# Differential attention: preparation of a half head in another order, weight loads over two tiles, a smaller descriptor scratch

## The chip, the cores and the metric

The kernel is one program on one core of a Trainium2 chip. The metric is the device time in microseconds of one execution. A kernel is executed several times; the time that counts is the median, and one further execution is recorded by the hardware profiler.

The engines are named as in the profile: PE is TensorE (matrix products, and transposes, which are products with an identity), DVE is VectorE, ACT is ScalarE, POOL is GpSimd, SP is SyncE, whose queue issues the transfers. PSUM is the memory that TensorE writes; it has eight banks, SBUF is the large on-chip memory.

## What is computed

One decoder layer on x of 1024 positions by 1024 channels, in float32. Three branches start from the same normalised h: an mLSTM, a differential attention and a cross-attention into 256 memory tokens. Each is projected to 1024 channels, multiplied by a sigmoid gate that is itself a projection of h, and summed; then an output projection and an MLP with squared ReLU. The change touches the differential attention and the gates:

```python
q = rms_norm(q, q_g); k = rms_norm(k, k_g)             # 8 heads, 2 components of 64 each
s = einsum('bhcqd,bhckd->bhcqk', q, k) * d ** -0.5     # causal
p = softmax(s)
a = p[:, :, 0] - lam * p[:, :, 1]                      # difference of the two components
o = einsum('bhqk,bhkv->bhqv', a, v)                    # v: 128 wide
o = rms_norm(o, subln_g) * (1 - lam_init)
g_m, g_d, g_c = split(sigmoid(h @ w_gate + b_gate), 3)
```

## The kernel before

Every float32 product is made of three products of a cheaper kind: both operands are split into a high part (a cast on ScalarE) and a low part (a subtraction on VectorE, L112), and high x high, high x low, low x high are added in one PSUM bank (`mm3`). Transposes go through PSUM in the same way, and their results are split as they are read out.

The program runs in stages: cross-attention, mLSTM, three passes of gates alone, the differential attention (`branch_d`, some 570 to 1190 us), the rest of the gates, and then output projection and MLP. TensorE's order in `branch_d` is written out by hand: all its instructions are kept in program order (`pin`), and the order on the other engines follows from the scheduler's priorities. The work is woven by a generator. `d_gemm` yields after each **step**, which is one of the eight 128-row slices k of a projection tile: three matmuls of 128x384. A tile is 128 positions of a head's q, k and v; four tiles are a half head (512 positions), and 16 half heads are 64 tiles. The loop of `branch_d` runs over 64 **attention steps** s, one block of 128 queries each. Each s makes two groups of scores (`sc`, one per component), the combination, the transposes of the block before (`tp`), and the product with the values (`po`) of the block before that. Between these pieces `fill(n)` puts n steps of projection, eight per s. When the projections are exhausted, `fill` takes gate steps instead.

After four tiles of a half head, `prep` returns five pieces with due times, in steps of the next half head. Each turn piece is four transposes (`pr` in the profile) into the *other* of the two banks `mm`, the one that the next tile will accumulate in; a cast on ScalarE and a subtraction on VectorE empty it (q: L866/L867, k: L880/L881). The piece `s_` (L874) scales the keys by their reciprocal norms on VectorE; it needs GpSimd's power of `drr` (L127, L128), which takes the sums of squares of the whole half head (L935). The line that gives the due times:

```python
return [(4, lambda: q_(0)), (12, lambda: q_(1)), (14, s_), (20, lambda: k_(0)), (28, lambda: k_(1))]
```

Each four s end with a normalisation (`norm`) in three parts: sums of squares and GpSimd's power of `dso`; the scaling on VectorE (L1054); four transposes and the result's store.

Weights of the next head are loaded and split during the last two tiles of its predecessor (`wload`, `wsplit`). Gate weights come through `gate_load` (L438 and L111/L112); the pools `wpg` (9 weight tiles) and `rpg` (2 raw tiles) serve both.

## Time and profile before

| quantity | value |
|---|---|
| median of three runs | 2282.28 us (2277.75, 2282.28, 2282.55) |
| profiled execution | 2277.11 us, span 2275.3 us |
| mean granted TensorE clock | 0.991 |
| busy: TensorE / VectorE / ScalarE / GpSimd | 2196.4 / 1395.3 / 1009.0 / 529.2 us |
| DMA queues with the kernel's data | q1 and q10, both hardware_dynamic: 233.36 and 12.58 MB |

The span is the time from the first to the last instruction. TensorE is busy in 97% of it, so its idle time, and the places where its clock is below 1, are what to look for. In a row of the timeline the bracket at the end is the idle time of that engine just before the row, and the instruction on whose end it waited. A busy time says nothing of the clock; the windows give that as a share of full speed (2.4 GHz; 0.5 is 1.2 GHz).

### The profile page before, as it was taken

The numbers are of one execution on the slowest core, as the hardware profiler recorded it, in microseconds if no ns is written. First come the engines' busy times: TensorE is split into PE (matmuls) and PEld (weight loads), VectorE is DVE, ScalarE is ACT, GpSimd is POOL, SyncE is SP. The second block draws the span as 40 slices with busy tenths as digits, with TensorE's granted clock in tenths as the row PEclk, the third lists the DMA queues.
The fourth block names the chain that finished last, engine by engine and source line by source line (L and its number), as shares of the span: only waits on it lengthen the run. The fifth ranks groups of instructions, "written<-read, shape, count | busy, mean of one in ns | idle before, by whom it ended". The sixth has DMA issues, their size and how long they took to land.

```text
span 2275.3 us, 30567 instructions
## 1 busy us (share of the span) xinstructions
PE 2196.4 (97%) x11222; PEld 1881.3 (83%) x11222; DVE 1395.3 (61%) x2627; ACT 1009.0 (44%) x1994; POOL 529.2 (23%) x696
## 2 busy tenths in 40 slices
PE   7999999999999999999899999999999999899999
PEld 5788789888899899999787888888787888688887
DVE  6636457552147877777662124353588877867789
ACT  6533445543246666666553202223345444543332
POOL 2100000000011101111000001111466766455553
PEclk9999999999999999999999999999999999999999
DMA  6022212201221100111125235434625444764444
GB/s 243 24 80 98 86 46 81 82 29 56 98 65 33 38 26 23 32 38 33 33 91 196 88 102 176 135 115 155 206 88 199 162 153 153 268 205 148 152 153 166
DMA packets 113781, 247.90 MB, mean 109 GB/s; under 512 B 11065, under 2 KB 19550, under 8 KB 111582
## 3 DMA queue, kind: packets, MB, share of 16 engines
q1 hardware_dynamic: 111326, 233.36, 30.6%
q10 hardware_dynamic: 2304, 12.58, 1.3%
q8 instruction: 88, 1.44, 0.3%
q14 instruction: 63, 0.52, 0.1%
HBM read 178.76 MB, written 67.14 MB: 108 GB/s over the span
## 4 chain that ended last, share of the span: by engine, by line
PE 73%; DVE 11%; DMA 7%; ACT 4%; issue 2%; POOL 2%; SPq 0%; DVEq 0%; ACTq 0%; POOLq 0%
PE mm L91 43%; PE p L91 21%; PE sc L91 5%; PE po L91 2%; PE tp L94 2%; ACT dpe L987 1%; DVE sc L979 1%; DVE w L112 1%; DMA raw<-in_wd 1%; DVE dpe L1000 1%; DVE daT L112 1%; DMA raw<-in_wgate 1%; DVE acc L67 1%; PE pr L94 1%; DVE dq L867 1%
## 5 line engine op out<-in xcount | busy, mean ns | idle before, releaser
L91 PE MATMUL mm<-w,hT 128*128 128x384 f32 (+3 forms) x2496 | 473.8, 331 | 13.3 <-DVE dq L867 8.7
L91 PE MATMUL mm<-hT,w 128*128 128x512 f32 x1920 | 470.4, 399 | 8.2 <-ACT w L111 6.1
L91 PEld LDWEIGHTS mm<-hT,w 128*128 128x128 f32 x1920 | 359.5, 191 | 85.1 <-ACT w L111 7.2
L91 PEld LDWEIGHTS mm<-w,hT 128*128 128x128 f32 x2496 | 387.5, 189 | 32.7 <-DVE dq L867 13.4
L91 PE MATMUL p<-xd,wo 128*128 128x512 f32 x1344 | 309.4, 392 | 5.8 <-DVE c L67 2.8
L91 PE MATMUL p<-xo,wo 128*128 128x512 f32 x1344 | 308.3, 390 | 6.0 <-DVE st L1397 1.8
L91 PEld LDWEIGHTS p<-xd,wo 128*128 128x128 f32 x1344 | 253.3, 189 | 61.8 <-DVE c L67 3.7
L91 PEld LDWEIGHTS p<-xo,wo 128*128 128x128 f32 x1344 | 251.1, 188 | 61.8 <-DVE u L67 3.7
L112 DVE TENSOR_TENSOR w<-raw,w 128x256 fp32r<-128x256 f32 (+3 forms) x304 | 172.8, 589 | 163.9 <-ACT w L111 162.7
L91 PE MATMUL mm<-kt,w 128*128 128x512 f32 x1152 | 261.3, 389 | 0.0
L91 PEld LDWEIGHTS mm<-kt,w 128*128 128x128 f32 x1152 | 216.3, 188 | 44.8
L111 ACT CAST w<-raw 128x256 fp32r<-128x256 f32 (+3 forms) x304 | 154.1, 532 | 198.4 <-PE mm L91 130.9
L104 ACT CAST wo<-wraw 128x896 fp32r<-128x896 f32 x122 | 115.0, 945 | 213.3 <-PE p L91 117.2
L67 DVE TENSOR_TENSOR wo<-wraw,wo 128x896 fp32r<-128x896 f32 x122 | 143.4, 1193 | 54.5 <-ACT wo L104 54.5
L1124 POOL TENSOR_TENSOR wraw<-wraw 128x128 f32<-128x128 f32 x128 | 92.9, 726 | 244.8 <-DMA wraw<-in_wup 86.2
L987 ACT ACTIVATE dpe<-sc,dst,drr 128x256 f32<-128x256 f32 (+7 forms) x128 | 106.7, 834 | 93.9 <-DVE dst L983 91.9
L979 DVE CUSTOM_DVE_ANT_0 sc<-sc,tmask 128x256 f32<-128x256 f32 (+7 forms) x128 | 96.9, 757 | 16.5 <-PE sc L91 16.5
L127 POOL TENSOR_SCALAR drr<-drr 128x16 f32<-128x16 f32 x16 | 3.6, 226 | 397.4 <-DVE drr L935 397.4
L1126 POOL TENSOR_TENSOR wraw<-wraw 128x128 f32<-128x128 f32 x128 | 92.2, 720 | 0.0
L1127 POOL TENSOR_TENSOR wraw<-wraw 128x128 f32<-128x128 f32 x128 | 87.2, 682 | 10.0
L127 POOL TENSOR_SCALAR hss<-hss 128x4 f32<-128x4 f32 x8 | 3.3, 409 | 356.8 <-ACT mscr L747 236.9
L91 PEld LDWEIGHTS po<-dv,daT 128*128 128x128 f32 x576 | 75.6, 193 | 11.7 <-DVE daT L112 10.2
(281 smaller groups left out, 3079.8 us busy)
## 6 DMA issues: line engine op xcount, KB each, us to landing
wraw<-in_wup SPq DMA_DIRECT2D x64, 256.0 KB, 2.9
r_d<-xts SPq DMA_DIRECT2D x16, 1024.0 KB, 4.1
wraw<-in_wdown SPq DMA_DIRECT2D x64, 256.0 KB, 3.1
xd<-r_d SPq DMA_DIRECT2D x19, 768.0 KB, 7.0
xd<-r_d SPq DMA_DIRECT2D x14, 1024.0 KB, 6.4
raw<-in_wgate SPq DMA_DIRECT2D x48, 256.0 KB, 2.8
gates<-gt SPq DMA_DIRECT2D x48, 256.0 KB, 2.0
raw<-in_wd SPq DMA_DIRECT2D x32, 384.0 KB, 3.1
```

The costliest lines, as they stand in the source:

```text
L67: return self.tc.keep_in_program_order(f(*a, **k))
L91: self.pin(self.nc.tensor.matmul(out, l, r, start=start, stop=stop))
L94: self.pin(self.nc.tensor.transpose(out, x, self.ident))
L104: self.A.copy(hi, src)
L111: nc.scalar.copy(hi, src)
L112: nc.vector.tensor_sub(lo, src, f32(hi))
L867: V.scalar_tensor_tensor(out=qT[lo, c], in0=pt[lo], scalar=self.gd[lo], in1=f32(qT[lo, c]), op0=ALU.mult, op1=ALU.subtract)
L979: V.tensor_tensor_reduce(out=sc[:, 0:n], in0=sc[:, 0:n], in1=self.tmask[:, D - n : D], scale=1.0, scalar=-3.0e38, op0=ALU.add, op1=ALU.max ...
L987: nc.scalar.activation(pe[c][:, 0:n], sc[:, 0:n], AF.Exp, bias=t8[:, 2 + c : 3 + c], scale=rr[:, i, c : c + 1], accum_out=t8[:, 4 + c : 5 ...
L1124: G.tensor_add(r[:, 4], r[:, 0], r[:, 3])
L1126: G.tensor_sub(r[:, 6], r[:, 1], r[:, 0])
L1127: G.tensor_sub(r[:, 7], r[:, 2], r[:, 5])
```

## The change

1. `gate_load` is called at every odd step of the third and fourth quarter of a pass instead of at every step of the fourth (L462).
2. `prep` has another order and other due times: first query turn at 4, scaling at 5, first key turn at 11, second query turn at 19, second key turn at 27. Tiles are handed to the attention with the first key turn. The attention starts after 60 steps instead of 64, half an attention step earlier against the tiles, and its loop runs one s longer.
3. A head's weights: three loads at the second tile's first step and a fourth after the second split; splits at the odd steps of the last two tiles. The last half head calls `gate_load` there instead.
4. At the end of the projections the remaining pieces are popped between 32 gate steps, by their due times; before, one after the other with nothing between.
5. `norm` parts 1 and 2 come one s later.
6. `wpg` has 13 buffers, `rpg` 3; the program is built with a descriptor scratch of 1024 bytes.

```diff
--- before.py
+++ after.py
@@ -459,7 +459,7 @@
                     ps = self.mm_tile()
                     for k in range(NK):
                         self.mm3(ps, (w[k][0][:, c], w[k][1][:, c]), (self.hT[:, k, 0, s], self.hT[:, k, 1, s]), k == 0, k == NK - 1)
-                        if q == 3 and r < run - 1:
+                        if q >= 2 and k % 2 and r < run - 1:
                             self.gate_load()
                         self.gdone = (g * 4 + q) * NK + k + 1
                         if k < NK - 1:
@@ -879,10 +879,10 @@
                     self.transpose(pt[:, i * P : (i + 1) * P], raws[i][:, 2 + c].rearrange("p a d -> p (a d)"))
                 nc.scalar.copy(kd[:, c], pt)
                 V.tensor_sub(kl[:, c], pt, f32(kd[:, c]))
-                if c == 1:
+                if c == 0:
                     kv.append((qT, kd, kl, vh, rr))
 
-            return [(4, lambda: q_(0)), (12, lambda: q_(1)), (14, s_), (20, lambda: k_(0)), (28, lambda: k_(1))]
+            return [(4, lambda: q_(0)), (5, s_), (11, lambda: k_(0)), (19, lambda: q_(1)), (27, lambda: k_(1))]
 
         raw = {}
 
@@ -893,19 +893,23 @@
             raw[hd, k + 1] = r[:, 384:768]
 
         def wsplit(hd, k, w):
-            if k % 2 == 0 and k < 6:
-                wload(hd, k + 2)
             t = self.wp.tile([P, 2, 384], F32R, tag="w", name=self.name("w"))
             self.split(t[:, 0], t[:, 1], raw.pop((hd, k)))
             w[k] = (t[:, 0], t[:, 1])
-
+            if k == 1:
+                wload(hd, 6)
+
+        nw = {}
         for j in range(16):
             hd, hf = divmod(j, 2)
             if j == 0:
-                w = {}
                 wload(0, 0)
+                wload(0, 2)
+                wload(0, 4)
                 for k in range(NK):
-                    wsplit(0, k, w)
+                    wsplit(0, k, nw)
+            if hf == 0:
+                w, nw = nw, {}
             rr = pool.tile([P, 4, 4], F32, tag="drr", name=self.name("drr"))
             vh, raws = [], []
             for i in range(4):
@@ -915,10 +919,14 @@
                     s = slice(t * P, (t + 1) * P)
                     self.mm3(ps, (self.hT[:, k, 0, s], self.hT[:, k, 1, s]), w[k], k == 0, k == NK - 1)
                     if hf and hd < 7:
-                        if i == 2 and k == 0:
+                        if i == 1 and k == 0:
                             wload(hd + 1, 0)
-                        if i == 3:
-                            wsplit(hd + 1, k, w)
+                            wload(hd + 1, 2)
+                            wload(hd + 1, 4)
+                        if i >= 2 and k % 2 == 1:
+                            wsplit(hd + 1, i % 2 * 4 + k // 2, nw)
+                    elif hf and i >= 2 and k % 2 == 1:
+                        self.gate_load()
                     while late and late[0][0] <= i * NK + k:
                         late.pop(0)[1]()
                     if k < NK - 1:
@@ -939,9 +947,11 @@
             self.rsqrt_mean(rl, rl, 64, 16)
             late = prep(raws, rr, vh)
             assert j < 4 or done[0] >= (j // 2 - 1) * 8
-        while late:
+        for n in range(NK * 4):
+            next(self.gates)
+            while late and late[0][0] <= n:
+                late.pop(0)[1]()
             yield True
-            late.pop(0)[1]()
 
     def branch_d(self, pool):
         nc = self.nc
@@ -1060,8 +1070,8 @@
                 nc.scalar.activation(y, pt, AF.Copy, scale=self.gsub)
                 self.store_y(1, hh // 2, hh % 2, y)
 
-        fill(64)
-        for s in range(NS + 3):
+        fill(60)
+        for s in range(NS + 4):
             hh, i = divmod(s - 2, 4)
             if s < NS:
                 scores(s, 0)
@@ -1072,12 +1082,12 @@
                     norm(hh, 0)
             if s < NS:
                 fill(2)
-            if s >= 6 and i == 1:
+            if s >= 6 and i == 2:
                 norm(hh - 1, 2)
             if s < NS:
                 scores(s, 1)
                 fill(1)
-            if s >= 6 and i == 0:
+            if s >= 6 and i == 1:
                 norm(hh - 1, 1)
             if 1 <= s < NS + 1:
                 turn(s - 1, 0)
@@ -1650,7 +1660,7 @@
                             return p.tile(shape, dt, tag=tag, name=name)
                     self.gpool, self.gwp, self.grp = T3(), self.wp, self.rp
                     self.branch_m(T3(), gm, 1)
-                with tc.tile_pool(name="wpg", bufs=9) as self.wp, tc.tile_pool(name="rpg", bufs=2) as self.rp:
+                with tc.tile_pool(name="wpg", bufs=13) as self.wp, tc.tile_pool(name="rpg", bufs=3) as self.rp:
                     self.gwp, self.grp = self.wp, self.rp
                     with tc.tile_pool(name="pg", bufs=2) as self.gpool:
                         for _ in range(3 * 32):
@@ -1730,7 +1740,7 @@
     from concourse.bass_utils import run_bass_kernel_spmd
 
     w = pack({k: np.asarray(v) for k, v in inputs.items()})
-    nc = bacc.Bacc("TRN2", target_bir_lowering=False, num_devices=1)
+    nc = bacc.Bacc("TRN2", target_bir_lowering=False, num_devices=1, dynamic_dma_scratch_size=1024)
     arrays, args = {}, {}
     for k, v in w.items():
         v = np.ascontiguousarray(v)
```

In the order of the built program: TensorE in one tile of the last but one head. `mm` is a projection step (x3: three matmuls), `pr` the turns of query or key, `tp` the turns of probabilities, `sc` scores, `po` the value product. Before, from the last of four turns on:

```order
L94 MATMUL pr_11040<-ident,draw_10815 128x128
L94 MATMUL tp_11048<-ident,dpe_10900 128x128 x2
L91 MATMUL mm_11012<-w_10781,hT 128x384 x3
L91 MATMUL mm_11012<-w_10794,hT 128x384 x3
L91 MATMUL sc_11066<-dk_10424,dq_10423 128x512
L91 MATMUL sc_11066<-dkl_10425,dq_10423 128x512
L91 MATMUL mm_11012<-w_10812,hT 128x384 x3
L91 MATMUL mm_11083<-w_10701,hT 128x384 x3
L91 MATMUL mm_11083<-w_10707,hT 128x384 x3
L91 MATMUL po_11090<-dv_10172,daT_11051 128x256
```

After, from the last of four turns on to the next tile:

```order
L94 MATMUL pr_11055<-ident,draw_10824 128x128
L91 MATMUL mm_11024<-w_10751,hT 128x384 x3
L91 MATMUL mm_11024<-w_10779,hT 128x384 x3
L91 MATMUL po_11068<-dv_10201,daT_11031 128x256
L91 MATMUL po_11068<-dv_10201,daT_11031 128x128
L91 MATMUL po_11068<-dv_10270,daT_11031 128x256
L91 MATMUL po_11068<-dv_10270,daT_11031 128x128
L91 MATMUL mm_11024<-w_10795,hT 128x384 x3
L91 MATMUL mm_11024<-w_10821,hT 128x384 x3
L91 MATMUL sc_11089<-dk_10441,dq_10440 128x512
L91 MATMUL sc_11089<-dkl_10442,dq_10440 128x512
L91 MATMUL mm_11095<-w_10645,hT 128x384 x3
```

The turn is followed by four steps, two matmul pairs of po and the scores before the next tile (another mm number) begins; before, it was three steps, the scores and tp. The transposes of the probabilities now stand behind a tile's first step.

TensorE at the end of the projections. `mm<-hT,w` with 128x512 is a step of a gate. Before:

```order
L91 MATMUL sc_11575<-dk_11168,dq_11167 128x128
L91 MATMUL sc_11575<-dkl_11169,dq_11167 128x128
L94 MATMUL pr_11581<-ident,draw_11242 128x128
L94 MATMUL pr_11581<-ident,draw_11338 128x128
L94 MATMUL pr_11581<-ident,draw_11429 128x128
L94 MATMUL pr_11581<-ident,draw_11527 128x128
L94 MATMUL tp_11588<-ident,dpe_11415 128x128 x4
L94 MATMUL pr_11596<-ident,draw_11242 128x128
L94 MATMUL pr_11596<-ident,draw_11338 128x128
L94 MATMUL pr_11596<-ident,draw_11429 128x128
L94 MATMUL pr_11596<-ident,draw_11527 128x128
L91 MATMUL mm_11635<-hT,w_11605 128x512 x3
```

After:

```order
L91 MATMUL mm_11595<-hT,w_11432 128x512 x3
L91 MATMUL sc_11627<-dk_11185,dq_11184 128x256
L91 MATMUL sc_11627<-dkl_11186,dq_11184 128x256
L91 MATMUL mm_11595<-hT,w_11456 128x512 x3
L91 MATMUL mm_11595<-hT,w_11493 128x512 x3
L94 MATMUL pr_11639<-ident,draw_11263 128x128
L94 MATMUL pr_11639<-ident,draw_11352 128x128
L94 MATMUL pr_11639<-ident,draw_11459 128x128
L94 MATMUL pr_11639<-ident,draw_11568 128x128
L91 MATMUL mm_11595<-hT,w_11521 128x512 x3
```

Before, the last groups of turns had only scores and one tp between them, and the gates began behind them; now the gates have begun, and the next group of turns stands behind their fifth step.

VectorE in the fourth tile of the second half of a head, where the next heads' weights are split (`w`). `daT` are the transposed probabilities, `dpe` of L1000 (now L1010) the combination of a block. Before:

```order
L112 TENSOR_TENSOR daT_10031<-tp_10026,daT_10031 128x512
L112 TENSOR_TENSOR w_10037<-raw_9984,w_10037 128x384
L112 TENSOR_TENSOR daT_10044<-tp_10040,daT_10044 128x384
L112 TENSOR_TENSOR w_10050<-raw_10014,w_10050 128x384
L1000 SCALAR_TENSOR_TENSOR dpe_9929<-dpe_9930,dst_9931,dpe_9929 128x1024
L983 SCALAR_TENSOR_TENSOR dst_10058<-dst_10058,drr_9340 128x1
L112 TENSOR_TENSOR w_10068<-raw_10014,w_10068 128x384
```

After:

```order
L112 TENSOR_TENSOR daT_10001<-tp_9996,daT_10001 128x512
L993 SCALAR_TENSOR_TENSOR dst_9918<-dst_9918,drr_8955 128x1
L112 TENSOR_TENSOR daT_10014<-tp_10010,daT_10014 128x384
L989 ISA sc_10026,dst_10025<-sc_10026,tmask 128x128
L989 ISA dst_10025 128x1
L112 TENSOR_TENSOR w_10035<-raw_9799,w_10035 128x384
L993 SCALAR_TENSOR_TENSOR dst_10025<-dst_10025,drr_9363 128x1
L112 TENSOR_TENSOR w_10051<-raw_9933,w_10051 128x384
L1006 RECIPROCAL dst_9918<-dst_9918 128x2
L112 TENSOR_TENSOR w_10077<-raw_9933,w_10077 128x384
L1007 SCALAR_TENSOR_TENSOR dst_9918<-dst_9918,dv 128x1
L1010 SCALAR_TENSOR_TENSOR dpe_9916<-dpe_9917,dst_9918,dpe_9916 128x1024
```

The subtractions of daT stood between those of w just ahead of the combination; they now stand ahead of the splits and of the combination (`dpe_9916`), and the key's low part (`dkl`) follows it.

## Rows read from the trace of the kernel before

**Rows 1.** The page, busy us of each engine (share of the span) xinstructions.

```profile
PE 2196.4 (97%) x11222; PEld 1881.3 (83%) x11222; DVE 1395.3 (61%) x2627; ACT 1009.0 (44%) x1994; POOL 529.2 (23%) x696
```

**Rows 2.** Windows, 660 to 1076: busy us per engine, then clock, DMA share, GB/s.

```profile
660.00:1076.00 416.00, 399.59 (x2550) 377.40 (x2550) 324.41 (x898) 261.59 (x636) 59.70 (x52) 1.00 0.12 34
```

**Rows 3.** Waits of TensorE, 660 to 1076: waiter <- releaser, us, times, longest.

```profile
PE mm L91 <- DVE dq L867: 8.7, 13, 0.9
PE po L91 <- DVE daT L112: 4.0, 12, 0.5
PE mm L91 <- DVE dkl L881: 2.8, 8, 0.6
PE pr L94 <- DVE dv L112: 1.0, 1, 1.0
```

**Rows 4.** Timeline of TensorE: start, duration, line, tiles, count [idle before <-releaser].

```profile
1052.11 0.60 PE L94 MATMUL pr<-ident,draw 128*128 128x128 f32 x4
...
1052.57 1.31 PE L91 MATMUL mm<-w,hT 128*128 128x384 f32 x6
...
1055.62 1.32 PE L91 MATMUL mm<-w,hT 128*128 128x384 f32 x6 [0.86 <-DVE dq L867]
1056.77 0.34 PE L91 MATMUL po<-dv,daT 128*128 128x256 f32 x2
```

**Rows 5.** Timeline of VectorE, the same stretch.

```profile
1054.22 0.69 DVE L1054 TENSOR_TENSOR doS<-doS,dso 128x512 f32<-128x512 f32 x1 [1.34 <-POOL dso L128]
1054.83 0.74 DVE L867 SCALAR_TENSOR_TENSOR dq<-pr,dv,dq 64x512 fp32r<-64x512 f32 x1
```

**Rows 6.** Timeline of TensorE, end of the projections.

```profile
1103.07 0.33 PE L94 MATMUL pr<-ident,draw 128*128 128x128 f32 x1 [1.48 <-ACT draw L927]
1103.16 1.80 PE L91 MATMUL po<-dv,daT 128*128 128x256 f32 x14
1105.18 0.66 PE L94 MATMUL pr<-ident,draw 128*128 128x128 f32 x4 [0.22 <-DVE dq L867]
...
1108.29 1.39 PE L94 MATMUL pr<-ident,draw 128*128 128x128 f32 x4 [2.27 <-DVE draw L874]
...
1111.35 1.12 PE L94 MATMUL pr<-ident,draw 128*128 128x128 f32 x4 [0.82 <-DVE dkl L881]
1113.87 1.65 PE L91 MATMUL mm<-hT,w 128*128 128x512 f32 x3 [1.40 <-DVE dkl L881]
```

**Rows 7.** Timeline of VectorE, the same stretch.

```profile
1103.93 0.41 DVE L935 TENSOR_REDUCE drr<-dscr 128x4 f32<-128x256 f32 x1
...
1105.16 1.09 DVE L112 TENSOR_TENSOR w<-raw,w 128x256 fp32r<-128x256 f32 x3
...
1107.72 1.43 DVE L874 TENSOR_TENSOR draw<-draw,drr 128x256 f32<-128x256 f32 x4 [0.22 <-POOL drr L128]
```

**Rows 8.** Timeline of GpSimd, the same stretch.

```profile
1104.79 2.90 POOL L128 TENSOR_TENSOR drr<-drr,mhalf 128x16 f32<-128x16 f32 x1
```

**Rows 9.** Windows at the two dips of the clock.

```profile
1112.00:1118.00 6.00, 4.60 (x16) 3.51 (x15) 1.38 (x2) 1.17 (x2) 0.00 (x0) 0.50 0.00 0
1118.00:1124.00 6.00, 6.00 (x33) 5.19 (x32) 1.00 (x4) 1.59 (x4) 0.00 (x0) 0.88 0.00 0
1242.00:1246.00 4.00, 3.79 (x10) 3.00 (x11) 1.43 (x4) 1.42 (x5) 0.00 (x0) 0.57 0.41 144
```

**Rows 10.** Timeline of TensorE, gates after the attention.

```profile
1215.88 8.47 PE L91 MATMUL mm<-hT,w 128*128 128x512 f32 x36 [0.45 <-ACT w L111]
1225.05 14.12 PE L91 MATMUL mm<-hT,w 128*128 128x512 f32 x60 [0.70 <-ACT gt L468]
1242.20 8.02 PE L91 MATMUL mm<-hT,w 128*128 128x512 f32 x27 [3.03 <-ACT w L111]
```

**Rows 11.** Timeline of ScalarE, the same stretch.

```profile
1241.75 1.36 ACT L111 CAST w<-raw 128x256 fp32r<-128x256 f32 x4 [4.16 <-DMA raw<-in_wgate]
```

**Rows 12.** GpSimd's power by tile drr: ns min/median/max, first and last start.

```profile
L128 POOL TENSOR_TENSOR drr<-drr,mhalf x16: 2898/2900/3306, 648.5 to 1104.8; 128x16 f32<-128x16 f32 x16
```

## The prediction, made before the changed kernel was run

> **What bounds the kernel now.** I read the page from the top. TensorE is busy 2196.4 of the span of 2275.3 us [rows 1]: time can come only from stretches in which it idles or runs at the lower clock, since the change neither adds nor removes a matmul. So I went to TensorE alone, in the places the diff touches.
>
> The steady part of the attention, 660 to 1076 us, is 416 us long. TensorE is busy 399.59 us there [rows 2], so 16.4 us are idle, in 6.6 pairs of half heads (the sixteen half heads take eight pairs; a pair lasts some 63 us), or 2.5 us a pair. The table of waits names what ended them [rows 3]: 8.7 us on VectorE's second half of the query (13 times), 4.0 on the transposed probabilities (12), 2.8 on the low part of the keys (8), 1.0 once on the low part of a value tile.
>
> One such wait in full. The four query transposes start at 1052.11, two projection steps, a score and a third step follow, and the next projection tile starts at 1055.62 after 0.86 idle: its PSUM bank is the one the transposes wrote, and VectorE has not read it out [rows 4]. VectorE is late because in its queue ahead of that read stands the normalisation at L1054, which sat 1.34 us waiting for GpSimd's power; the read ran from 1054.83 for 0.74 [rows 5]. Chain: transposes, ScalarE, VectorE, next tile.
>
> At the end of the projections (tile 64 of 64) there is no projection left between the five pieces of preparation, and the code pops them with empty steps. The waits there [rows 6] are 1.48 + 2.27 + 0.82 + 1.40 = 6.0 us. The 2.27 is the longest: VectorE's scaling of the keys (L874) starts at 1107.72 [rows 7], as soon as GpSimd's 2.90 us power from 1104.79 [rows 8] is done. The idleness brings the clock down: the granted clock is 0.50 in 1112 to 1118 (the 1.2 GHz level) and 0.88 in the six after [rows 9], against 1.00 in the steady part [rows 2].
>
> In the gates that follow the attention three waits stand, 0.45 + 0.70 + 3.03 = 4.2 us [rows 10]; the long one waits for ScalarE's cast of a gate weight, which itself waited 4.16 us for its transfer [rows 11]; the code asks for all loads of a pass in its last quarter. The clock dips to 0.57 in the 4 us after it [rows 9].
>
> **The change part by part.**
>
> Steady part. What changes per projection tile is the cover between the four transposes and the next tile, which needs their bank. Before it is three projection steps, one score and a transpose. The built order shows now, in three tiles of four, four steps, a score and the value product po. Two steps take 1055.62 to 1056.77 = 1.15 us [rows 4], so a step is 0.57; po has 2 to 16 matmuls, and one of 14 on TensorE at 1103.16 kept the next group back to 1105.18 [rows 6], so up to some 2 us. Each wait on the query or the keys is thus covered by 0.6 to over 2 us more, and the 0.86 above by all but 0.3 us or less. The normalisation at L1054 comes one attention step (eight projection steps, some 6 us) later, so its 1.34 us head-of-line wait ends: the power is done before VectorE asks. The probabilities: on VectorE daT now stands ahead of the combination (L1010, was L1000), and between transposes and po there is also one pr group more; their 4.0 us should go. What is late next: with the transposes moved up to steps 3 and 4 of a tile, the bank they write must have been read out by ScalarE and VectorE from the tile before (the dv wait of [rows 3]), about 0.35 us a pair; in the tile of the first query only three steps cover, and in the shortest score tiles the keys come late, some 0.75 a pair together. I put 1.1 us a pair in place of 2.5, so 6.6 x 1.1 = 7.3 remain of 16.4: **gain 9.1**. Bounds: all 16.4 goes; or the new order makes as many new stalls and half a microsecond a pair more, -4.
>
> The weight splits. The code asks for them at odd steps of the last two tiles, but the built order puts all eight casts and subtractions of a head's weights in one tile still (three for the next head, five for the one after). ScalarE and VectorE work there beside TensorE as before; VectorE is the busiest in those tiles. Cost taken as 0; if cover is short there it shows as daT or dkl waits, and is inside the bounds above. The three loads of a head are now issued together, one tile earlier, on SP's queue, which then waits for nothing the steady part needs: 0.
>
> End of the projections. The five pieces now run at steps 4, 5, 11, 19 and 27 of 32 gate steps. These gate steps ran later before; at 0.7 us each (worked out below) they fill what was empty. Between the transposes of one piece and the next use of the bank lie three to five gate steps, 2 to 3.5 us, against a chain of some 1.6 us. The 2.27 us on GpSimd goes too: the scaling is behind five gate steps (3.5 us) plus the transposes, sc and tp. All 6.0 us go, and with them the clock dip: busy 4.60 us at half speed is 2.3 us, 6.00 at 0.88 is 0.7, and about half a microsecond before 1112 [rows 9], 3.5 in all. **Gain 9.5**; bounds 5 (the dip stays with one wait of 2 us) to 10. It needs the gates' weights to be there: the last half head loads eight of them in its last two tiles, in place of a next head's.
>
> Gates after the attention. Loads start in the third quarter of a pass, and three raw buffers and 13 weight buffers stand where two and nine did. A gate step is three matmuls, 8.47/12 = 0.7 us [rows 10], and a quarter is eight steps, so the first transfers of a pass are asked for 8 x 0.7 = 5.6 us earlier; the one that kept ScalarE 4.16 us [rows 11] then comes in time. The 3.03 and the 0.45 go; the 0.70 on ScalarE's tanh may stay in part; the dip gives 3.79 x 0.43 = 1.6 us [rows 9]. **Gain 5.4**; bounds 2 to 6.
>
> Gates before the attention: the first load is still behind the same buffer of the pool before, and the spreading in their passes meets no wait; counted as 0. Norm transposes at the very end: 0. Descriptor scratch of 1 KB: the page's two queues that carry the kernel's data are both of the hardware kind, and GpSimd issues no transfer in the program, so 0; it only makes the room for the buffers.
>
> Sum: 9.1 + 9.5 + 5.4 = 24.0. The profiled execution took 2277.11 us (span 2275.3), so 2253.1. The three timed runs are 2277.75, 2282.28 and 2282.55: they sit at the profiled time or 5 above it, and the change can come out at either. I say 2254.
>
> **A rule against the change.** The scaling s_ is moved from step 14 to step 5, close behind GpSimd's power, which must be done first. In the row, the power took 2.90 us with three subtractions of two SBUF operands on VectorE beside it [rows 7, 8]. The Trainium skill (SBUF — State Buffer, section "Who interferes with whom") says that a VectorE instruction with two SBUF inputs contends with a GpSimd instruction that reads SBUF, because both use the shared read interface. By that rule the power would stretch where the splits are gathered, and the rival below would be likelier; the trace does not agree: the sixteen powers take 2.898 to 3.306 us with a median of 2.900 [rows 12], so the one beside the subtractions is at the lower end.
>
> **The rivals.**
> - The steady part does not move: what the built order does with the splits says that the spreading is not what was written, and the gathered tile makes as many late reads as are saved. For it: VectorE queues are long there. Against: the waits by name [rows 3] are not on splits. Then 2277.1 - 9.5 - 5.4 = 2262.
> - All the steady waits go: 2277.1 - 16.4 - 9.5 - 5.4 = 2246. For it: every cover is longer. Against: the bank must be free two pieces earlier in a tile.
> - Slower: s_ at step 5 waits on VectorE for the power, with the next score's maximum and what follows queued behind it, in each of 15 half heads. For it: L935 starts some 1.5 us after the tile's last matmul (the transposes at 1103.07 waited 1.48 for ScalarE's copy of the same tile, [rows 6]) and the power ends 3.8 us after L935 began [rows 7, 8], so 5.3 us into the new tile; five steps (2.9), two groups of transposes (0.45 each, from 1052.11 to 1052.57, [rows 4]), and the two reads of the query (VectorE's 0.74 of [rows 5], ScalarE's taken as equal) bring VectorE to s_ at 5.3, plus a score. The margin is about nothing, and less where the splits make L935 late. If each half head then pays what the same wait cost at the end, 2.27 us, that is 15 x 2.27 = 34, and 2253.1 + 34 = 2287. It decides from 24.0 / 15 = 1.6 us a half head. Against: in the built order the query's read-out stands ahead of s_, and behind it only a maximum, for which TensorE does not wait at once; a VectorE wait of one microsecond there costs TensorE nothing.
>
> **How the numbers follow.** Forecast 0.55, steady part unmoved 0.18, all waits gone 0.14, slower by s_ 0.08, and 0.05 that the three gains together are under 5 us. A measurement of this kernel can tell about 0.2%, 4.6 us, from no change. Faster: the first three, with the upper level of the runs, 0.86; same 0.06; slower 0.08. The forecast alone has 2246 to 2260. The range for 8 in 10 takes in the unmoved steady part at the upper level (2262 + 5) and all waits gone less a little: 2242 to 2268.
>
> **What would show it.** In the profile after: no wait longer than about 0.5 us on dq in the attention and L1064 without a wait on GpSimd; no stall over 1 us between the last projection and the gates, with the clock at 1.00 there; no 3 us wait on a gate weight after the attention; TensorE's idle time in 416 us of the steady part near 7 us. I am wrong if VectorE waits for drr at L874 in every half head, if waits on dv or dkl take the place of those on dq, or if the dip only moves.

## The result and the profile after

The changed kernel takes 2240.65 us (median of 5 runs, 2236.63 to 2243.3) where the one before took 2282.28: a ratio of 0.982, with a 95% interval of 0.9805 to 0.9835. The forecast was 2254 us with a range of 2242 to 2268. The direction was right; the time lies 1.35 us below the range, since the gain is 38 to 42 us and not 24 to 28. Profiled execution against profiled execution it is 2277.11 to 2238.88, or 38.2 us. In three groups of runs further down (turns one step earlier, start at 64, old splits) one execution was slow, at 3626, 4399 and 3004 us; the ratios leave it out, and the median without it is lower by 0.3 us at most.

I split both traces at three marks: ScalarE's copy of the first projection tile, its copy of the sixty-fourth, and the first matmul of the output projection. The windows between the marks, first of before (start to end, width, then busy time of PE, PEld, DVE, ACT, POOL, then TensorE's clock, share and rate of the DMA engines):

```profile
634.20:1102.40 468.20, 450.77 (x2863) 426.36 (x2861) 354.62 (x975) 288.14 (x699) 64.02 (x56) 1.00 0.11 33
1102.40:1284.70 182.30, 170.85 (x793) 140.66 (x794) 70.81 (x164) 69.64 (x143) 6.97 (x8) 0.94 0.32 107
```

and of after:

```profile
635.20:1084.50 449.30, 444.95 (x2873) 427.49 (x2873) 350.70 (x977) 291.11 (x700) 62.63 (x56) 1.00 0.11 33
1084.50:1246.00 161.50, 159.21 (x786) 132.96 (x785) 65.95 (x156) 66.31 (x135) 6.83 (x8) 1.00 0.33 111
```

The projections lose 18.9 us of width and the rest of attention and gates 20.8. What precedes takes 1.0 us more, what follows 0.5 (991.1 against 990.6), so 38.2 remain. Of the 18.9, 13.1 is idle time of TensorE (17.4 to 4.35); of the 20.8, 9.2 is idle (11.45 to 2.29). The rest, 5.8 and 11.6 us, is busy time, for the same matmuls. I had expected busy time to fall by the clock alone.

The waits of TensorE in the projections, which answer to [rows 3] (waiter, releaser, us in total, times, longest):

```profile
PE pr L94 <- DVE dst L993: 2.0, 5, 0.4
PE tp L94 <- ACT yd L1070: 1.7, 5, 0.4
PE mm L91 <- DVE dq L867: 0.6, 1, 0.6
```

Waits on the query fell from 8.7 to 0.6, those on daT and dkl are gone; in their place 3.7 us have come on a small scaling of VectorE (dst) and on ScalarE's read-out of a result (yd). The end of the projections, as [rows 6] before:

```profile
1084.81 0.90 PE L91 MATMUL mm<-hT,w 128*128 128x512 f32 x3
...
1088.06 1.55 PE L91 MATMUL mm<-hT,w 128*128 128x512 f32 x6
1089.45 0.60 PE L94 MATMUL pr<-ident,draw 128*128 128x128 f32 x4
1089.80 0.94 PE L91 MATMUL mm<-hT,w 128*128 128x512 f32 x3
```

No bracket stands in it: gate steps and turns alternate without a wait, and the clock in that stage is 1.00 where it was 0.94. After the attention, where [rows 10] has three waits, TensorE has none up to the output projection at 1245.98:

```profile
1160.85 85.30 PE L91 MATMUL mm<-hT,w 128*128 128x512 f32 x375
```

What about VectorE and GpSimd? VectorE's longest sum of waits on GpSimd, and the power by tile (ns min/median/max):

```profile
DVE doS L1064 <- POOL dso L128: 2.7, 6, 0.5
```

```profile
L128 POOL TENSOR_TENSOR drr<-drr,mhalf x16: 2900/2902/2908, 649.4 to 1086.2; 128x16 f32<-128x16 f32 x16
```

The normalisation still waits, 0.5 us where it was 1.34 [rows 5]; the scaling at L874 waits for no power at all in the projections, so the slower rival did not come about. The power takes 2.900 to 2.908 us in all sixteen half heads, where [rows 12] goes up to 3.306. In the trace of before the five longest (2.988 to 3.306 us) all ran beside weight splits (L112 on w) or the combination of VectorE, which have two operands in SBUF, and the eight without such work beside them took 2.898 to 2.902; in the trace of after splits and combinations stand beside the power too, and none is stretched.

One thing explains the busy time of the projections. A projection step behind a score takes 0.53 us up to the next instruction when that one can start, and 0.69 when it cannot. Of these rows of before the first two show a step ahead of a stall, the other two one without (the stall's own 0.86 is apart from it):

```profile
1054.07 0.69 PE L91 MATMUL mm<-w,hT 128*128 128x384 f32 x3
1055.62 1.32 PE L91 MATMUL mm<-w,hT 128*128 128x384 f32 x6 [0.86 <-DVE dq L867]
...
1058.40 0.69 PE L91 MATMUL mm<-w,hT 128*128 128x384 f32 x3
1058.93 0.60 PE L94 MATMUL pr<-ident,draw 128*128 128x128 f32 x4
```

1055.62 - 0.86 - 1054.07 = 0.69, and 1058.93 - 1058.40 = 0.53: the last matmul's tail is covered by its successor, or counted as busy when there is none. So this stall costs some 0.16 us beyond its idle time. Before had 35 stalls in this stage, after 11, which is 24 x 0.16 = 3.9 of the 5.8 us. The kernels of the next section that have no dip of the clock in this stage say more: TensorE's busy time in it is 444.4 us with 7 stalls (the last one), 447.9 with 21 (before + buffers) and 451.9 with 35 (before + new tail), 0.2 to 0.3 us a stall, by which the 24 make up all of the 5.8.

### The profile page after: what moved, and what is told of

Its sections match the earlier page's. It is cut to its first block, busy times and chain, and to the rows that moved or that the text cites. A ratio compares the mean times of both kernels' runs of the same rounds, so it can differ in the third digit from the quotient of the medians.

```text
span 2237.1 us, 30556 instructions
## 1 busy us (share of the span) xinstructions
PE 2180.2 (97%) x11222; PEld 1875.4 (84%) x11222; DVE 1394.6 (62%) x2627; ACT 1012.0 (45%) x1994; POOL 534.1 (24%) x696
## 4 chain that ended last, share of the span: by engine, by line
PE 78%; DVE 8%; DMA 5%; ACT 4%; issue 2%; POOL 1%; SPq 0%; DVEq 0%; ACTq 0%; POOLq 0%
PE mm L91 46%; PE p L91 21%; PE sc L91 6%; PE tp L94 2%; PE po L91 2%; PE pr L94 1%; DVE w L112 1%; DVE acc L67 1%; DMA raw<-in_wd 1%; DVE u L67 1%; DVE wo L67 1%; DMA kraw<-y 1%; ACT dpe L997 1%; ACT w L111 0%; DVE c L67 0%
## 5 line engine op out<-in xcount | busy, mean ns | idle before, releaser
L91 PE MATMUL mm<-w,hT 128*128 128x384 f32 (+3 forms) x2496 | 480.7, 332 | 2.6 <-ACT w L111 1.7
L91 PE MATMUL mm<-hT,w 128*128 128x512 f32 x1920 | 464.7, 396 | 2.8 <-ACT w L111 2.6
L91 PEld LDWEIGHTS mm<-w,hT 128*128 128x128 f32 x2496 | 385.8, 189 | 14.9 <-ACT w L111 2.4
L112 DVE TENSOR_TENSOR w<-raw,w 128x256 fp32r<-128x256 f32 (+3 forms) x304 | 171.9, 589 | 141.0 <-ACT w L111 139.7
L104 ACT CAST xd<-xd 128x1536 fp32r<-128x1536 f32 (+2 forms) x36 | 54.9, 1528 | 69.8 <-DMA xd<-r_d 69.7
```

Source lines behind the costliest of these rows:

```text
L91: self.pin(self.nc.tensor.matmul(out, l, r, start=start, stop=stop))
L104: self.A.copy(hi, src)
L112: nc.vector.tensor_sub(lo, src, f32(hi))
```

## The experiments

All were timed in five rounds beside the kernel before, whose median in the four groups was 2277.4, 2278.3, 2278.2 and 2277.3 us. The changed kernel was timed in none of these groups, so its distance to a variant is best taken from the ratios and the profiles. "Projections" is the first stage above, with TensorE's idle time in it, "rest" the second, both from the profile.

| kernel | median us | ratio, 95% interval | projections us (idle) | rest us |
|---|---|---|---|---|
| before (profile) | 2282.28 | | 468.2 (17.4) | 182.3 |
| changed kernel | 2240.65 | 0.982, 0.9805 to 0.9835 | 449.3 (4.4) | 161.5 |
| before + transposes of probabilities apart | 2272.46 | 0.998, 0.997 to 0.999 | 465.1 (15.9) | 179.9 |
| before + turns one step earlier | 2265.56 | 0.9944, 0.9929 to 0.9958 | 457.9 (10.1) | 178.3 |
| before + later normalisation | 2288.42 | 1.0053, 1.0038 to 1.0069 | 480.9 (22.7) | 179.1 |
| before + new tail | 2263.25 | 0.9941, 0.9925 to 0.9957 | 468.7 (16.8) | 163.7 |
| before + new turns | 2274.57 | 0.9984, 0.9974 to 0.9993 | 462.4 (11.8) | 182.6 |
| before + buffers | 2259.03 | 0.992, 0.9906 to 0.9933 | 457.9 (10.0) | 171.6 |
| before + buffers + new splits | 2259.91 | 0.9926, 0.9913 to 0.9938 | 457.9 (10.0) | 171.8 |
| before + buffers + later normalisation | 2254.74 | 0.9906, 0.9894 to 0.9919 | 456.6 (9.9) | 172.3 |
| changed, old normalisation | 2245.97 | 0.9853, 0.9834 to 0.9872 | 452.3 (7.4) | 161.3 |
| changed, start at 64 | 2241.06 | 0.9834, 0.9815 to 0.9854 | 446.8 (2.1) | 162.4 |
| changed, old splits | 2240.61 | 0.9834, 0.9817 to 0.985 | 449.1 (4.3) | 161.5 |
| changed, old buffers | 2254.25 | 0.9896, 0.9879 to 0.9913 | 450.4 (5.4) | 171.6 |
| changed, old turns and start | 2247.14 | 0.9864, 0.9845 to 0.9882 | 456.6 (9.2) | 161.8 |
| the same, old normalisation too | 2247.6 | 0.9868, 0.9854 to 0.9882 | 457.8 (9.4) | 161.0 |
| changed, old gate loads | 2237.66 | 0.9829, 0.981 to 0.9847 | 449.0 (4.1) | 161.5 |
| changed, start at 64, end filled | 2232.58 | 0.9798, 0.978 to 0.9815 | 446.5 (2.1) | 159.7 |

**Transposes apart.** In the trace four turns take 0.43 us ahead of transposes and 0.35 ahead of a projection step. Is that worth something by itself?

```diff
             if s < NS:
                 scores(s, 1)
+            if 1 <= s < NS + 1:
+                turn(s - 1, 0)
+            if s < NS:
                 fill(1)
...
             if 1 <= s < NS + 1:
-                turn(s - 1, 0)
                 if s < NS:
                     fill(1)
```

> The kernel before, with the first group of probability transposes one projection step earlier, so that it no longer stands directly behind the four turns of a query or key (56 such pairs before, none here). Theory 1 (two groups of transposes in a row cost more than apart: a turn group takes 0.43 us ahead of transposes in the trace of before, 0.35 ahead of a projection step in the trace of after): 56 x 0.08 = 4.5 us faster than before, turn groups at 0.35 us. Theory 2 (that difference is only how the records of a group end): within 1 us of before apart from waits that move.

Measured: 0.2% faster, 3.1 us less in the projections. Turn groups did fall to 0.35 us:

```profile
1050.71 0.77 PE L91 MATMUL mm<-w,hT 128*128 128x384 f32 x3
1051.32 0.60 PE L94 MATMUL pr<-ident,draw 128*128 128x128 f32 x4
1051.67 1.29 PE L91 MATMUL mm<-w,hT 128*128 128x384 f32 x6
```

But the first row stands behind a transpose and takes 1051.32 - 1050.71 = 0.61 us, not 0.53: a step right behind transposes pays, and there are now two such steps instead of one (over the stage 141 runs of steps start right behind a group of transposes, where before had 86). Both cancel: theory 1 falls. What was gained is waits on daT, 4.2 us in this stage before and none here; those on query and keys rose by 2.4.

**Turns one step earlier.** Due times 3, 11, 14, 19, 27 in place of 4, 12, 14, 20, 28.

> The kernel before, with the four turns at steps 3, 11, 19 and 27 of the next half head instead of 4, 12, 20 and 28. Theory 1 (the cover behind a turn decides its wait, and turns apart from probability transposes are cheaper): one step of 0.57 us more cover on 21 waits of mean 0.55 us takes some 8 of the 11.5 us on query and keys, and the separation 4.5: 12 us faster. Theory 2 (the waits come from the normalisation ahead in VectorE's queue, whatever the cover): waits on the query shrink only by the step in half of the tiles, 3 to 5 us faster in all.

Measured: 12 us, as theory 1 has it, but only partly for its reason. The waits on query and keys went altogether, and new ones came:

```profile
PE po L91 <- ACT daT L111: 6.4, 6, 1.1
PE pr L94 <- DVE dv L112: 1.9, 2, 1.5
```

Cover decides the wait on the bank. ScalarE is now late for the probabilities in the tiles of the weight splits, where its cast of daT stands behind a split that waits for its transfer:

```profile
787.57 0.51 ACT L111 CAST w<-raw 128x384 fp32r<-128x384 f32 x1 [1.24 <-DMA raw<-in_wd]
...
789.18 0.46 ACT L111 CAST daT<-tp 128x384 fp32r<-128x384 f32 x1
```

**Later normalisation alone.** `norm` parts 1 and 2 at i == 1 and i == 2, loop to NS + 4.

> The kernel before, with parts 1 and 2 of the normalisation one attention step later, as in the change, and nothing else. Theory 1 (VectorE's 1.34 us wait for GpSimd stands ahead of the query's read-out in every second turn of a query): about half of the 8.7 us on the query goes, 3 to 5 us faster. Theory 2 (the cover alone decides): within 1.5 us of before.

Neither: 0.5% slower. The query's waits fell from 8.7 to 5.5 us, but not for the reason of theory 1. Though the code asks for it one attention step later, the scaling has kept its place on VectorE, right ahead of the query's read-out, and waits 1.3 us for GpSimd in six half heads, the same 8.1 us as in the trace of before:

```profile
DVE doS L1054 <- POOL dso L128: 8.1, 6, 1.3
```

What has moved is the combination (dpe). In a fourth tile, where weights are split, it and a split now stand ahead of daT:

```profile
984.08 1.28 DVE L1000 SCALAR_TENSOR_TENSOR dpe<-dpe,dst,dpe 128x1024 f32<-128x1024 f32 x1
985.28 0.55 DVE L112 TENSOR_TENSOR w<-raw,w 128x384 fp32r<-128x384 f32 x1
985.75 0.68 DVE L112 TENSOR_TENSOR daT<-tp,daT 128x512 fp32r<-128x512 f32 x1
```

In the kernel before, both subtractions of daT came first there (the last row is the next query's read-out):

```profile
969.65 0.28 DVE L112 TENSOR_TENSOR dv<-mm,dv 128x128 fp32r<-128x128 f32 x1
...
976.69 0.69 DVE L112 TENSOR_TENSOR daT<-tp,daT 128x512 fp32r<-128x512 f32 x1
977.29 0.55 DVE L112 TENSOR_TENSOR w<-raw,w 128x384 fp32r<-128x384 f32 x1
977.76 0.55 DVE L112 TENSOR_TENSOR daT<-tp,daT 128x384 fp32r<-128x384 f32 x1
978.23 0.55 DVE L112 TENSOR_TENSOR w<-raw,w 128x384 fp32r<-128x384 f32 x1
978.69 1.28 DVE L1000 SCALAR_TENSOR_TENSOR dpe<-dpe,dst,dpe 128x1024 f32<-128x1024 f32 x1
...
984.01 0.76 DVE L867 SCALAR_TENSOR_TENSOR dq<-pr,dv,dq 64x512 fp32r<-64x512 f32 x1
```

TensorE pays for it in two ways, by waits and by the clock that falls behind them:

```profile
PE po L91 <- DVE daT L112: 12.9, 13, 2.1
PE mm L91 <- DVE dq L867: 5.5, 8, 0.9
```

```profile
986.49 2.92 PE L91 MATMUL po<-dv,daT 128*128 128x256 f32 x14 [1.82 <-DVE daT L112]
```

```profile
986.90:990.30 3.40, 3.40 (x17) 3.40 (x17) 2.56 (x9) 1.19 (x5) 0.95 (x2) 0.50 0.61 136
```

Six such waits of 1.81 to 2.09 us stand in the trace, and behind five of them the clock is 0.50 for 3.4 to 6.8 us. The five dips hold 20 us (the stage's mean clock is 0.98), in which TensorE is busy throughout: some 10 us of busy time that the upper level would not need, where the projections lose 12.7 and the idle time grew by 5.2. The mean clock of the six runs is 0.985 to 0.990, against 0.988 to 0.994 in the seventeen runs of before beside them, so the other executions have lower clocks too.

**Tail alone.**

```diff
-        while late:
+        for n in range(NK * 4):
+            next(self.gates)
+            while late and late[0][0] <= n:
+                late.pop(0)[1]()
             yield True
-            late.pop(0)[1]()
```

> The kernel before, with the last five pieces of preparation popped between gate steps, as in the change, and nothing else; the gates' weights are not loaded ahead. Theory 1 (the gates need their weights ahead): the 6.0 us of waits and the dip of 3.5 us give way to one wait of 2 to 4 us on a weight's cast and a smaller dip, 3 to 6 us faster. Theory 2 (the gate steps alone fill the end): 9.5 us faster.

Measured: 14 us by the medians, 18.6 in the second stage by the profile, more than either theory. At the end of the projections the weights were there without the early loads; after the attention one wait of 1.6 us on a gate weight is left of the three in [rows 10]. The profile shows more: at the end of the attention two waits stand as before, and the clock stays up.

```profile
1176.04 1.17 PE L94 MATMUL tp<-ident,dpe 128*128 128x128 f32 x8 [0.82 <-DVE dpe L1002]
1178.13 2.06 PE L91 MATMUL po<-dv,daT 128*128 128x256 f32 x16 [0.92 <-DVE daT L112]
```

```profile
1106.50:1270.20 163.70, 159.75 (x791) 133.16 (x790) 71.23 (x164) 69.92 (x143) 7.41 (x8) 1.00 0.36 119
```

In the kernel before, the same two waits were followed by a dip, the second of three in that stage:

```profile
1179.19 1.16 PE L94 MATMUL tp<-ident,dpe 128*128 128x128 f32 x8 [0.83 <-DVE dpe L1000]
1181.27 3.14 PE L91 MATMUL po<-dv,daT 128*128 128x256 f32 x13 [0.92 <-DVE daT L112]
```

```profile
1109.20:1119.40 10.20, 7.97 (x25) 6.20 (x26) 3.98 (x11) 3.29 (x8) 0.00 (x0) 0.50 0.01 2
1180.90:1187.60 6.70, 6.33 (x23) 5.75 (x24) 1.95 (x5) 1.39 (x4) 0.00 (x0) 0.50 0.22 78
1242.30:1245.70 3.40, 3.40 (x8) 2.67 (x9) 1.31 (x4) 0.82 (x4) 0.00 (x0) 0.50 0.43 148
```

So before has 20.3 us at the lower level in that stage, with TensorE busy in 17.7 of them, which at the upper level would have been 8.9 us less; the tail kernel and the changed one have none. In three other kernels with the old tail (transposes apart, turns earlier, new turns) the junction (the end of the projections) dips, but the end of the attention does not. So a dip behind waits of 1.75 us comes in some profiles and not in others. One execution of each kernel was profiled: whether the dip in the profile of before (about 3 us) is chance is not shown.

**New turns alone.** The new list of due times in the kernel before.

> The kernel before with the new order and due times of the five pieces alone (start after 64 steps, handed over as before with the second key turn). Theory 1 (the turns alone carry the steady gain, the normalisation at its old place leaves some): 10 to 15 us faster than before, waits on dq and dkl nearly gone. Theory 2 (the parts need each other): under 6 us faster, with waits on daT in place of those on dq.

Theory 2: 0.16% faster. Waits on query and keys are gone, 7.8 us on daT and 3.3 on the turns have come; the projections gain 5.8.

**Old normalisation, start, splits, buffers,** each taken back alone in the changed kernel.

> The changed kernel with parts 1 and 2 of the normalisation back at their old places, one attention step earlier. Theory 1 (the later normalisation keeps VectorE from standing 1.3 us on GpSimd ahead of reads that TensorE waits for): that wait is back in each half head and costs TensorE some 0.5 us with its drain: 6 to 10 us slower than the changed kernel. Theory 2 (in the new phase nothing that TensorE wants soon stands behind it): within 2 us of the changed kernel.

5 us slower by the medians, 3.0 of it in the projections by the profile, though the two intervals just touch. It lies between the theories, and for another reason than theory 1 has: the turns wait 6.9 us in place of 2.0 on VectorE, but VectorE's wait for GpSimd is the same as in the changed kernel:

```profile
DVE doS L1064 <- POOL dso L128: 2.7, 6, 0.5
```

So the place in the code does not set this wait. In the kernel before with the new turns alone it is 1.2 us: it is the turns that brought it down from 8.1.

> The changed kernel with the attention starting after 64 steps again instead of 60, the turns' new order and due times kept. Theory 1 (the half step decides where probabilities' transposes and the value product fall between turn and next tile): waits of 0.5 us come back on daT or on the turns in most half heads: 6 to 12 us slower than the changed kernel. Theory 2 (the turns' due times alone do it): within 2 us of the changed kernel.

Theory 2: the start half an attention step earlier is worth nothing; without it TensorE idles 2.1 us in place of 4.35.

> The changed kernel with the loads of a head's weights at the third tile and the splits asked for at each step of the fourth, as before. Theory 1 (the built order gathers the splits in one tile anyway): within 2 us of the changed kernel. Theory 2 (asking over two tiles is what frees VectorE for the read-outs): 5 us slower or more, with waits on daT and dkl back in the tiles of the splits.

Theory 1: the new code of loads and splits moves nothing.

> The changed kernel with 9 weight buffers and 2 raw buffers again (the small descriptor scratch kept). Theory 1 (the gate loads asked for early need buffers to land in): waits on the cast of gate weights return, 2 to 4 us after the attention and some at the end of the projections: 3 to 8 us slower than the changed kernel. Theory 2 (asking earlier is enough): within 2 us.

Slower by 13.6 us, more than theory 1 has. The projections lose only 1.1 us; the rest loses 10. There are long waits on daT at the end of the attention (1.43 and then 0.60 us), where, as I read it, early gate loads without a free buffer hold up ScalarE and VectorE; the clock is 0.50 for 10.2 us from 1153.8 on, and the wait on the gate weight is back:

```profile
1152.85 0.79 PE L91 MATMUL po<-dv,daT 128*128 128x128 f32 x5 [1.43 <-DVE daT L112]
...
1216.85 3.46 PE L91 MATMUL mm<-hT,w 128*128 128x512 f32 x14 [2.78 <-ACT w L111]
```

**Old turns in the changed kernel.**

> The changed kernel with the old pieces at their old due times (4, 12, 14, 20, 28) and the start after 64 steps that they need; tail, weights, normalisation and pools as changed. Theory 1 (the turns' order and due times carry the gain of the steady part): some 15 us of the 18.9 come back there, about 13 to 18 us slower than the changed kernel. Theory 2 (weights, normalisation and buffers carry it): within 4 us of the changed kernel.

Neither theory: 6.5 us slower by the medians, 7.3 in the projections by the profile. The other parts together hold 11.6 of the 18.9. Taken back from the changed kernel, the buffers had cost the projections only 1.1; what do they do alone?

> The kernel before with 13 weight and 3 raw buffers (and the small scratch that makes room) alone. In its built order five splits of the next head but one come right behind the three of the next head, instead of waiting one by one for the buffer that the running tile gives back. Theory 1 (the buffers take the splits off the read-outs in VectorE's queue): 5 to 12 us of the steady part go, 3 more after the attention. Theory 2 (the buffers serve the gates only): within 2 us in the steady part, some 3 us after the attention.

Theory 1, and more: 0.8% faster, 18 us, the largest single part. The projections lose 10.3 us and the waits are

```profile
PE mm L91 <- DVE dq L867: 5.1, 6, 0.9
PE mm L91 <- DVE dkl L881: 2.5, 8, 0.3
PE po L91 <- DVE daT L112: 1.6, 7, 0.4
```

With nine buffers eight hold the running head's weights, so a split for the next head waits until the running tile gives one back, step by step, and seven splits stand in VectorE's queue between the read-outs dv of the third and the fourth tile, two of them around daT (the rows of before above). With thirteen five stand there, ahead of daT, and three in the next tile:

```profile
964.35 0.28 DVE L112 TENSOR_TENSOR dv<-mm,dv 128x128 fp32r<-128x128 f32 x1
...
971.32 0.55 DVE L112 TENSOR_TENSOR daT<-tp,daT 128x384 fp32r<-128x384 f32 x1
971.79 1.28 DVE L1000 SCALAR_TENSOR_TENSOR dpe<-dpe,dst,dpe 128x1024 f32<-128x1024 f32 x1
...
977.30 0.76 DVE L867 SCALAR_TENSOR_TENSOR dq<-pr,dv,dq 64x512 fp32r<-64x512 f32 x1
```

From the third tile's dv to the query's read-out it is 984.01 - 969.65 = 14.4 us in before and 977.30 - 964.35 = 13.0 here. That is 1.4 us in this head, 1.2 to 1.6 in each of the seven in which a next head's weights are split, and 10.1 in all: the 10.3 us. Weight and raw buffers were raised together, and ScalarE's waits for a head's weights to be transferred went as well (7.8 us in the projections of before, none here), so which of the two pools it takes is not shown. In the changed kernel seven splits stand between the two read-outs again; they cost little there, since both subtractions of daT are ahead of them.

The rest loses 10.7 us: no wait on gate weights after the attention, no dip at its end; the junction's dip stays (0.98).

```profile
1094.30:1265.90 171.60, 164.12 (x793) 135.78 (x794) 66.74 (x158) 66.17 (x137) 6.81 (x8) 0.98 0.31 102
```

> The kernel before with the buffers and the new code of loads and splits. Theory 1 (the built order of the splits is that of the buffers alone): within 2 us of the kernel with the buffers alone. Theory 2 (earlier loads free ScalarE of waits for transfers): 3 us or more faster than that.

Theory 1: 0.9 us apart, the same waits to the tenth.

> The kernel before with the buffers and the later normalisation. Theory 1 (the later normalisation cost 12.7 us because VectorE met it among the splits of the last tile, which the buffers now thin out): its loss goes, and with the buffers it is 3 us or more faster than the buffers alone. Theory 2 (its place in the old turns is bad in itself): some 10 us slower than with the buffers alone.

Nearer theory 1: the 12.7 us loss is gone, with the clock at 1.00 in the projections; against the buffers alone the intervals overlap. VectorE's wait for GpSimd is 8.1 us here as well.

> The changed kernel with the old pieces, the start after 64 steps and the normalisation at its old place. Theory 1 (the later normalisation is good in the new surroundings): 5 to 9 us slower than with the old pieces alone taken back, with the waits of before on dq. Theory 2 (neutral there): within 2 us of it.

Theory 2: with the old turns and the buffers the normalisation's place is neutral, as the 8.1 us of its wait are in both; it pays 3 to 5 us only with the new ones.

**Gate loads.** Asked for in the fourth quarter only, none ahead in the last half head, buffers kept.

> The changed kernel with gate loads asked for in the fourth quarter of a pass only, and none ahead in the last half head; 13 and 3 buffers kept. Theory 1 (with enough buffers the early asking is worth the waits it removes): a wait of 1 to 3 us on a gate weight is back after the attention, 2 to 5 us slower than the changed kernel. Theory 2 (the end of the projections needs its weights ahead): a further wait of 2 to 4 us there, 5 to 9 us slower.

Neither: not slower at all (2237.66 us). No wait on gate weights is back. With the buffers it goes without the earlier asking; without either, the new tail alone leaves 1.6 us of it.

**A faster version.** Start at 64, and at the end of the attention

```diff
             if s < NS:
                 scores(s, 0)
+            if s < NS + 2:
                 fill(3)
...
-            if s < NS:
+            if s < NS + 1:
                 fill(2)
...
             if s < NS:
                 scores(s, 1)
+            if s < NS + 1:
                 fill(1)
...
-                if s < NS:
-                    fill(1)
+                fill(1)
```

> The changed kernel with the start after 64 steps, and ten gate steps put between the last two blocks' transposes and value products, where the changed kernel has nothing to do. Theory 1: the waits of 0.9 and 1.0 us at the end of the attention go and the steady part idles 2 us instead of 4.7: 3 to 5 us faster than the changed kernel. Theory 2 (a chain of VectorE and ScalarE ends the attention whatever stands beside it): within 1.5 us of the changed kernel.

Theory 1, and some more: 2232.58 us, a ratio of 0.9798 to before. TensorE has no idle time at all in the second stage:

```profile
1080.90:1240.60 159.70, 159.70 (x799) 134.30 (x798) 67.44 (x159) 68.33 (x140) 6.80 (x8) 1.00 0.34 112
```

By the profile it gains 1.8 us there and 2.8 in the projections over the changed kernel; the 8 us between the medians come from two groups of runs and hold some difference of those, and the intervals of the two ratios overlap.

## Why the prediction was wrong

**The step that failed** is the first one: "time can come only from stretches in which it idles or runs at the lower clock". In the projections the clock is 1.00 in both kernels, and TensorE's busy time falls by 5.8 us all the same: a stall costs its idle time and 0.2 to 0.3 us of busy time, and there are 24 fewer. In the stage behind them busy time falls by 11.6 us, where I had 3.5 + 1.6 = 5.1 for the clock; by the three dips it was 8.9, and what the rest is stays open. Together busy time holds 5.8 + 6.5 = 12.3 of the 14.2 us that I missed.

**Steady part.** Forecast 9.1 for cover, order and normalisation; measured 18.9 for the whole projection stage, which is 26 us longer at either end than the stretch I summed: 13.1 of idle time and the 5.8. The cover did remove the waits, as the step had it: dq, dkl and daT are 0.6 us together. The remainder of 7.3 us of new waits was too much, 4.4 are left.

**The normalisation.** The step "comes one attention step (eight projection steps, some 6 us) later, so its 1.34 us head-of-line wait ends" is wrong. Written later in the code, the scaling stands where it stood on VectorE: the move alone leaves all 8.1 us of its wait, and taking it back leaves the 2.7 us of the changed kernel. The new turns shortened the wait, to 0.5 us at most. The move does pay with the new turns (3.0 us in the projections), through something that I have not found.

**The weight splits.** "Cost taken as 0" had no reason behind it either. I had seen in the built order that the splits change places and had not asked why: thirteen buffers in place of nine. Alone the buffers take 10.3 us from the projections, and I had given them a price at the gates only. But this is not what the forecast lacks: with all of the change but the buffers the projections take 450.4 us, 17.8 less than before. The buffers and the rest of the change largely end the same waits, and what one has gained the other cannot gain again. What brings the new turns from the 462.4 us that they reach alone to these 450.4 (the normalisation's place, the tail, the new splits, the start) is not told apart by any run.

**End of the projections.** All but 0.2 us of the waits and the dip went, as forecast. The size was low: the tail kernel, which has this part alone, gains 18.6 us in the stage, 7.5 of idle time (11.45 to 3.95) and 11.1 of busy time, which takes in the dips at the end of the attention and after it.

**Gates after the attention.** The waits and the dip went, the cause named was wrong: asking 5.6 us earlier is worth nothing with the buffers. Without them it seems to cost: the changed kernel with the old buffers takes 171.6 us in that stage, the new tail alone 163.7, though other parts differ too.

**Counted as 0.** The two waits at the end of the attention stayed, as I said (0.88 and 1.02 us after); the dip behind them did not come, worth some 3 us (6.33 us of busy time at the lower level). The new splits' code, the earlier loads and the start of the gates were 0. The scratch by itself was not run; it is part of every kernel with the larger buffers.

**The rivals.** "All the steady waits go" (2246) came nearest, by luck: 4.4 us of waits are left, and it priced busy time no better. "Steady part unmoved" was wrong in its reason too: the splits' places do matter. The slower rival needed VectorE to wait for the power at L874, and in the projections it never did. In the rule against the change I read the trace of before by one row; "the trace does not agree" holds for that row, but five of the eight powers beside splits or combinations were stretched, by up to 0.4 us. In the changed kernel none was.

**The sum.** Profile against profile: forecast 24.0, measured 38.2. Projections 18.9 in place of 9.1 make 9.8 of the difference (4.0 of idle time, 5.8 of busy time); the rest 20.8 in place of 14.9 makes 5.9 (busy time 6.5 more, idle time 0.6 less), and 1.5 lost outside takes it to 14.2.

## What to carry to other kernels

A pool that holds exactly one set of weights plus one buffer makes every load of the next set wait for the running one, step by step, and so decides the order on the engines that prepare them: price a change of buffer counts through that order, at each place where the pool is used. A piece that is written later in the code need not stand later on its engine: look it up in the built order before you price the move. Count a stall as its idle time plus the tail of the matmul before it. Waits of one to two microseconds were followed by a dip of the clock in some profiles and not in others, so price a dip as something that may come. Parts that look additive may not be: the later normalisation cost the projections 12.7 us in the old surroundings, most of it by the clock, gained 1.3 with more buffers and 3.0 with the new turns; the buffers gave them 10.3 us alone and 1.1 on top of the rest.

## What the runs showed of the hardware

Groups of transposes: four turns take 0.43 us when transposes follow and 0.35 when a projection step does, but that step then takes 0.61 in place of 0.53 to 0.55 behind scores. Separating the groups gains nothing by itself. A stall of TensorE costs 0.2 to 0.3 us beyond its idle time (444.4 us busy in the projections with 7 stalls, 451.9 with 35).

The same two waits of 0.82 to 0.83 and 0.92 us at the end of the attention were followed by 6.7 us at 0.50 in one trace and by a clock of 1.00 in another; of six waits of 1.81 to 2.09 us in the kernel with the later normalisation alone, five were followed by 3.4 to 6.8 us at 0.50. GpSimd's power on 128x16 took 2.900 to 2.908 us in the changed kernel. In the kernel before it took 2.988 to 3.306 in five of the eight half heads in which VectorE ran splits or combinations with two operands in SBUF beside it, and 2.898 to 2.902 in the other eight.
